# The even layer's q, k and convolution branch projected with the weight matrix as the stationary operand

## The chip, the cores and the metric

The kernel runs on one core of one Trainium2 chip. The metric is the time of one execution on the device in microseconds (us): the median of three runs of the kernel before is 798.65 us (798.03 to 799.74). A profiled execution gives a trace in which each engine's instructions stand with start and duration: PE (TensorE matmuls), PEld (TensorE loads of the stationary operand), DVE (VectorE), ACT (ScalarE), POOL (GpSimd) and SP (SyncE, which issues most of the transfers).

## The reference

Two layers act on 256 positions of width 2048. The even layer (the first) is the one that is changed:

```python
h = rms_norm(x, ev_norm_w[i])
proj = h @ w_in                              # 2048 -> 8192
q, k, v, g_ret, gate_b, gate_c, u, g_conv = jnp.split(proj, 8, axis=-1)   # 1024 columns each
q = rope(q.reshape(shp), pos)                # 4 heads of 256
k = rope(k.reshape(shp), pos)
o = retention_chunkwise(q, k, v.reshape(shp))
ret_out = rms_norm_nogain(o).reshape(b, s, RET_WIDTH) * jax.nn.silu(g_ret)
conv = lax.conv_general_dilated(gate_c * u, conv_w[:, None, :], ...)   # width 3, causal, per channel
conv_out = gate_b * conv * jax.nn.silu(g_conv)
return jnp.concatenate([ret_out, conv_out], axis=-1) @ w_out
```

The odd layer (RMS norm, a projection to 4608 columns, banded attention over 32 query heads with a gate, an output projection) is the same before and after.

## The kernel before

All inputs are float32. Every operand of a projection is split into two parts of the type float32r, a high one (a rounded copy) and a low one (what is left), and each product is made of three matmuls: high by high, high by low, low by high. The weights come from memory in pieces of 128 x 1024 float32 (two k-tiles of 512 columns). `Chunk.split` loads a piece (L164, issued by SP), makes the high part on ACT (L165, `wh`) and the low part on DVE (L166, `wl`). The activations, already split, lie in SBUF with features on the partitions: `a0h` and `a0l` are the normalised input of the even layer.

A `Chunk` is one block of 512 output columns: 16 k-tiles, two blocks of 128 positions, three products, so 96 matmuls (L143). In each, a 128 x 128 block of the activation is stationary and 512 columns of the weight piece move, so the result has positions on the partitions and 512 features beside them, in two PSUM tiles `ps..._0` and `ps..._1`, one for each block of positions. The even layer's input projection is 16 chunks, in the order of the table

```python
EVEN_ORDER = [4, 0, 2, 6, 5, 1, 3, 7, 10, 12, 14, 8, 11, 13, 15, 9]
```

where column block c belongs to kind c // 2 (0 q, 1 k, 2 v, 3 retention gate, 4 gate_b, 5 gate_c, 6 u, 7 g_conv) and half c % 2. After them come four chunks of the even output projection (`eo`), nine of the odd input projection (`okv`, `oq`, `og`) and four of the odd output projection (`oo`).

PE's instructions stand in the order in which the code makes them, except that a layer below may move one by a few rows. A chunk is fed piece by piece (`feed`), and after each piece one step of the queue `pending` is put in: work of the layer's other parts (rope, retention, convolution), written as generators. So short bursts of other PE work stand between the pieces of the projections.

`even_done` takes a finished chunk out of PSUM. Row scaling by `r0` (the RMS norm, one number for each position) is done there: ACT scales v and the gates on the way out (L383), DVE multiplies u by gate_c and gate_b by the gate (L387). For q and k, DVE makes the rope with tables that were multiplied by `r0` beforehand (L252), with positions on the partitions. But retention needs q and k with features on the partitions, and so does the convolution, which runs along positions. So `rope_turn` (L277) transposes each rope result on PE in four 128 x 128 pieces and ACT copies it to SBUF (L278), and `conv` transposes both of its inputs (`yt` L345, `bt` L362), which DVE then reads from PSUM. These transposes are matmuls with the identity (part of the table `cst`).

Of the kernel before, what the change touches and what calls it, by code (L numbers as in the profile page):

```python
# [8 lines left out]
F32 = mybir.dt.float32  # L9
F32R = mybir.dt.float32r  # L10
AF = mybir.ActivationFunctionType
ALU = mybir.AluOpType
# [3 lines left out]
P = 128  # L16
D = 2048
S = 256
T = S // P
KT = D // P  # L20
N = 512
PK = 2
NP = KT // PK
EPS = 1e-6
RH, RD = 4, 256
HD = 64
# [15 lines left out]
C_ROPE1 = C_LOWER + P  # L42
C_END = C_ROPE1 + T * 128
E_ROPE0 = 0
E_MASK = E_ROPE0 + T * 512
E_END = E_MASK + RH * 384

S_NW0 = 0
# [9 lines left out]
def hybrid_kernel(  # L58
# [13 lines left out]
    nc = tc.nc  # L72
# [4 lines left out]
    tw = ctx.enter_context(tc.tile_pool(name="tw", bufs=W2_BUFS))  # L77
    mm = ctx.enter_context(tc.tile_pool(name="mm", bufs=4, space=PSUM))
    tp = ctx.enter_context(tc.tile_pool(name="tp", bufs=2, space=PSUM))
    at = ctx.enter_context(tc.tile_pool(name="at", bufs=2, space=PSUM))  # L80

    cst = cp.tile([P, C_END], F32, tag="cst", name="cst")
# [43 lines left out]
    class Chunk:  # L126
# [30 lines left out]
        def split(self, pc, fine=False):  # L157
# [8 lines left out]
                nc.vector.tensor_tensor(out=wl[:, ws], in0=raw[:, ws], in1=f32(wh[:, ws]), op=ALU.subtract)  # L166
            return wh, wl

    def stage(chunks, done):

        q = 3 * NP // 4
        a, b = Chunk(*chunks[0]), Chunk(*chunks[1])
        a.feed(0, q)
        b.feed(0, q)
        drain()
        a.feed(q, NP)
        done(0, a.ps)
        b.feed(q, NP)
        done(1, b.ps)
        for n in range(2, len(chunks)):  # L180
            c = Chunk(*chunks[n])
            c.feed(0, NP)
            done(n, c.ps)
# [43 lines left out]

    with tc.tile_pool(name="e", bufs=1) as ep, tc.tile_pool(name="e2", bufs=2) as ep2:
        cst0 = ep.tile([P, E_END], F32, tag="cst0", name="cst0")
        rope0 = cst0[:, E_ROPE0 : E_ROPE0 + T * 512].rearrange("p (t a d) -> p t a d", t=T, a=2)  # L230
        r0 = cp.tile([P, T], F32, tag="r0", name="r0")
        ssx = cp.tile([P, T, 4], F32, tag="ssx", name="ssx")

# [12 lines left out]
            nc.vector.tensor_copy(r0, r)  # L246

        def load_tables():
            nc.sync.dma_start(out=cst0[:, :E_MASK], in_=const0[:, :E_MASK])
            for t in range(T):  # L250
                rt = cst0[:, E_ROPE0 + t * 512 : E_ROPE0 + (t + 1) * 512]
                nc.vector.tensor_scalar(out=rt, in0=rt, scalar1=r0[:, t : t + 1], scalar2=None, op0=ALU.mult)  # L252

        cact = Act("c0")

        def rope_pair(name, ps, dst):

            for t in range(T):
                v = ps[t].rearrange("p (h s d) -> p h s d", h=2, s=2)
                a = tw.tile([P, 2, 2, P], F32, tag="w2", name=f"ra{name}{t}")  # L260
                b = tw.tile([P, 2, 2, P], F32, tag="w2", name=f"rb{name}{t}")
                cs = rope0[:, t, 0].unsqueeze(1).broadcast_to([P, 2, 256])
                nc.vector.tensor_tensor(
                    out=a.rearrange("p h s d -> p h (s d)"),
                    in0=ps[t].rearrange("p (h d) -> p h d", h=2), in1=cs, op=ALU.mult,
                )
                for s in range(2):
                    sn = rope0[:, t, 1, s * P : (s + 1) * P].unsqueeze(1).broadcast_to([P, 2, P])
                    nc.vector.tensor_tensor(out=b[:, :, s, :], in0=v[:, :, 1 - s, :], in1=sn, op=ALU.mult)
                af = a.rearrange("p h s d -> p (h s d)")  # L270
                nc.vector.tensor_tensor(out=af, in0=af, in1=b.rearrange("p h s d -> p (h s d)"), op=ALU.add)
                pending.append(rope_turn(f"{name}{t}", af, dst[:, :, t * P : (t + 1) * P]))

        def rope_turn(name, a, dst):
            tr = tp.tile([P, 4, P], F32, tag="tp", name=f"rt{name}")
            for j in range(4):
                nc.tensor.transpose(tr[:, j, :], a[:, j * P : (j + 1) * P], ident)  # L277
            nc.scalar.activation(dst, tr, AF.Copy)  # L278
            yield

        def retention(i, qT, kT, v, sg):
            ch, cl = cact.new()
# [55 lines left out]
        def conv(i, y, bg):  # L338
            yield
            ch, cl = cact.new()  # L340
            for c in range(0, 4, 2):
                yt = tp.tile([P, 2, S], F32, tag="tp", name=f"yt{i}{c}")
                for j in range(2):
                    for t in range(T):
                        nc.tensor.transpose(  # L345
                            yt[:, j, t * P : (t + 1) * P], y[:, t, (c + j) * P : (c + j + 1) * P], ident
                        )
                a = tw.tile([P, 2, S], F32, tag="w2", name=f"ca{i}{c}")
                for j in range(2):
                    o = S_CONV + (4 * i + c + j) * 3  # L350
                    nc.vector.tensor_scalar(
                        out=a[:, j, :], in0=yt[:, j, :], scalar1=sml[:, o + 2 : o + 3], scalar2=None, op0=ALU.mult
                    )
                    for d in (1, 2):
                        nc.vector.scalar_tensor_tensor(
                            out=a[:, j, d:], in0=yt[:, j, : S - d], scalar=sml[:, o + 2 - d : o + 3 - d],
                            in1=a[:, j, d:], op0=ALU.mult, op1=ALU.add,
                        )
                bt = tp.tile([P, 2, S], F32, tag="tp", name=f"bt{i}{c}")
                for j in range(2):  # L360
                    for t in range(T):
                        nc.tensor.transpose(  # L362
                            bt[:, j, t * P : (t + 1) * P], bg[:, t, (c + j) * P : (c + j + 1) * P], ident
                        )
                nc.vector.tensor_tensor(out=a, in0=bt, in1=a, op=ALU.mult)
                ks = slice(c, c + 2)
                nc.scalar.activation(ch[:, ks, :], a, AF.Copy)
                nc.vector.tensor_tensor(out=cl[:, ks, :], in0=a, in1=f32(ch[:, ks, :]), op=ALU.subtract)
                yield
# [4 lines left out]
        def even_done(n, ps):  # L374
            kind, i = EVEN_ORDER[n] // 2, EVEN_ORDER[n] % 2
            if kind in (0, 1):
                dst = ep.tile([P, 4, S], F32, tag="qk"[kind], name=f"{'qk'[kind]}T{i}")
                rope_pair(f"{kind}{i}", ps, dst)
                keep[kind] = dst
            elif kind in (2, 3, 5, 7):  # L380
                dst = ep.tile([P, T, N], F32, tag={2: "v", 3: "g", 5: "v", 7: "g"}[kind], name=f"e{kind}{i}")
                for t in range(T):
                    nc.scalar.activation(  # L383
                        dst[:, t, :], ps[t], AF.Silu if kind in (3, 7) else AF.Copy, scale=r0[:, t : t + 1]
                    )
                keep[kind] = dst
                if kind == 3:  # L387
                    pending.append(retention(i, keep[0], keep[1], keep[2], keep[3]))
            else:
                dst = ep.tile([P, T, N], F32, tag="q" if kind == 6 else "k", name=f"e{kind}{i}")  # L390
                for t in range(T):
                    nc.vector.scalar_tensor_tensor(
                        out=dst[:, t, :], in0=ps[t], scalar=r0[:, t : t + 1],
                        in1=keep[5 if kind == 6 else 7][:, t, :], op0=ALU.mult, op1=ALU.mult,
                    )
                keep[kind] = dst
                if kind == 4:
                    pending.append(conv(i, keep[6], keep[4]))

        for n, c in enumerate(EVEN_ORDER):  # L400
            if n == 0:
                continue
            ch = Chunk(f"e{c}", w0, n, act0)
            if n == 1:
                ch.feed(0, 1)
                load_x(0)
                ch.feed(1, 3)
                load_x(1)
                ch.feed(3, 5)
                stats()  # L410
                even_done(0, ch0.ps)
                load_tables()
                ch.feed(5, 6)
                nc.sync.dma_start(out=cst, in_=const1)
                nc.vector.tensor_copy(identr, ident)
                ch.feed(6, NP)
                nc.sync.dma_start(out=cst0[:, E_MASK:], in_=const0[:, E_MASK:])
            else:
                ch.feed(0, NP)
            even_done(n, ch.ps)  # L420
# [401 lines left out]
def _constants():  # L822
# [3 lines left out]
    e, c = np.zeros((P, E_END), f), np.zeros((P, C_END), f)  # L826
    c[:, C_ID : C_ID + P] = np.eye(P, dtype=f)

    def rope(dst, o, d):
        inv = f(1.0) / (10000.0 ** (np.arange(0, d, 2) / d)).astype(f)  # L830
        a = (np.arange(S, dtype=f)[:, None] * inv[None, :]).astype(np.float64)
        cos, sin = np.cos(a).astype(f), np.sin(a).astype(f)
        full = np.concatenate([cos, cos, -sin, sin], 1)
        for t in range(T):
            dst[:, o + 2 * d * t : o + 2 * d * (t + 1)] = full[t * P : (t + 1) * P]

    rope(e, E_ROPE0, RD)
    rope(c, C_ROPE1, HD)
    j = np.arange(P)[:, None]
    i = np.arange(S)[None, :]  # L840
    for h in range(RH):
# [58 lines left out]
```

## Time and profile before

| | |
|---|---|
| median of three runs | 798.65 us |
| the profiled execution's own time | 798.12 us |
| its span, first to last instruction | 796.4 us |
| PE busy | 789.2 us, 99% of the span |
| weight loads (PEld) busy | 652.4 us, 82% |
| DVE busy | 500.0 us, 63% |
| ACT busy | 419.9 us, 53% |
| granted TensorE clock | full (1.0) throughout |

The page's busy time of PE counts an engine as busy while any matmul is in flight. Matmuls overlap: a 128 x 512 one lasts some 390 ns in the trace, while the next one starts some 227 ns after it. What a matmul costs is therefore the distance between starts, not the duration, and this is read from the timeline or from the chain of waits, where each piece is a run of instructions of one line with its length and count.

### The profile page before, as it was taken

To read this page: it belongs to the slowest core of one execution; us is meant where nothing else is said; L and a number is where in the kernel's file an instruction comes from. 1 tells how busy PE (TensorE), PEld (TensorE's weight loads), DVE (VectorE), ACT (ScalarE), POOL (GpSimd) and SP (SyncE) were. 2 spreads that over 40 slices of the span, in tenths; PEclk is the share of its full clock that TensorE was granted. 3 is DMA by queue.
4 is the path that set the end of the run, shared out by engine and by line. 5 is a ranking of instruction groups with operands and counts; after the bars stand their busy time and mean duration, and the time that the engine had idled before them with its cause. 6 is when DMAs were issued, how large, how long until landed. Compare 5 with 4: busy or idle time off the path is not lost.

```text
span 796.4 us, 10004 instructions
## 1 busy us (share of the span) xinstructions
PE 789.2 (99%) x3660; PEld 652.4 (82%) x3660; DVE 500.0 (63%) x742; ACT 419.9 (53%) x665; POOL 61.7 (8%) x61
## 2 busy tenths in 40 slices
PE   8999999999999999999999999999999999999998
PEld 5888888888888888888888888888888888888886
DVE  6676444664544475545857664877988877877651
ACT  6843444443444434343345444658758678686430
POOL 0000000000000000000000000330410501401000
PEclk9999999999999999999999999999999999999999
DMA  8966545555455555655555555463463464445750
GB/s 298 418 240 228 197 140 184 185 188 196 137 187 188 198 184 181 201 185 195 176 191 179 186 185 187 136 216 97 158 216 133 134 207 158 146 146 184 229 168 26
DMA packets 41088, 147.09 MB, mean 185 GB/s; under 512 B 4560, under 2 KB 4944, under 8 KB 40784
## 3 DMA queue, kind: packets, MB, share of 16 engines
q1 hardware_dynamic: 40752, 146.23, 54.3%
q8 instruction: 28, 0.46, 0.2%
q10 hardware_dynamic: 288, 0.24, 0.2%
q14 instruction: 20, 0.16, 0.1%
HBM read 144.36 MB, written 2.10 MB: 184 GB/s over the span
## 4 chain that ended last, share of the span: by engine, by line
PE 96%; POOL 1%; DVE 1%; DMA 1%; issue 0%; SPq 0%; ACT 0%; DVEq 0%; POOLq 0%
PE pse L143 44%; PE pseo L143 11%; PE psoo L143 11%; PE psoq L143 10%; PE psog L143 10%; PE psokv L143 3%; PE pt L675 1%; DMA we<-in_w 1%; PE ov L698 1%; PE ov L697 1%; POOL rq L225 1%; PE qt L598 1%; PE s L607 0%; PE s L610 0%; PE s L609 0%; PE gt L666 0%
## 5 line engine op out<-in xcount | busy, mean ns | idle before, releaser
L166 DVE TENSOR_TENSOR wle<-we,whe 128x1024 fp32r<-128x1024 f32 (+1 forms) x129 | 156.2, 1217 | 147.6 <-ACT whe L165 147.4
L165 ACT ACTIVATE whe<-we 128x1024 fp32r<-128x1024 f32 (+1 forms) x129 | 135.4, 1052 | 172.8 <-PE pse L143 160.5
L143 PE MATMUL pse<-whe,a0h 128*128 128x512 f32 x512 | 199.4, 394 | 1.4 <-ACT whe L165 1.4
L143 PE MATMUL pse<-whe,a0l 128*128 128x512 f32 x512 | 197.5, 390 | 0.0
L143 PE MATMUL pse<-wle,a0h 128*128 128x512 f32 x512 | 197.4, 389 | 0.0
L143 PEld LDWEIGHTS pse<-whe,a0h 128*128 128x128 f32 x512 | 95.8, 188 | 23.1 <-ACT whe L165 3.9
L143 PEld LDWEIGHTS pse<-whe,a0l 128*128 128x128 f32 x512 | 96.1, 188 | 20.5
L143 PEld LDWEIGHTS pse<-wle,a0h 128*128 128x128 f32 x512 | 96.2, 188 | 19.4
L165 ACT ACTIVATE wheo<-weo 128x1024 fp32r<-128x1024 f32 x32 | 33.9, 1061 | 48.3 <-PE pseo L143 32.7
L166 DVE TENSOR_TENSOR wleo<-weo,wheo 128x1024 fp32r<-128x1024 f32 x32 | 39.2, 1225 | 27.5 <-ACT wheo L165 27.5
L166 DVE TENSOR_TENSOR wloo<-woo,whoo 128x1024 fp32r<-128x1024 f32 x32 | 38.9, 1225 | 26.9 <-ACT whoo L165 26.7
L165 ACT ACTIVATE whoo<-woo 128x1024 fp32r<-128x1024 f32 x32 | 33.9, 1062 | 40.3 <-PE psoo L143 32.7
L165 ACT ACTIVATE whoq<-woq 128x1024 fp32r<-128x1024 f32 x32 | 34.0, 1063 | 36.3 <-PE psoq L143 14.0
L166 DVE TENSOR_TENSOR wloq<-woq,whoq 128x1024 fp32r<-128x1024 f32 x32 | 38.9, 1223 | 19.2 <-ACT whoq L165 18.7
L143 PE MATMUL psog<-whog,a1h 128*128 128x512 f32 x128 | 50.9, 398 | 0.0
L143 PE MATMUL psoq<-whoq,a1h 128*128 128x512 f32 x128 | 50.8, 397 | 0.0
L143 PE MATMUL pseo<-wheo,c0h 128*128 128x512 f32 x128 | 50.8, 397 | 0.0
L143 PE MATMUL psog<-wlog,a1h 128*128 128x512 f32 x128 | 50.0, 391 | 0.5 <-DVE wlog L166 0.5
L143 PE MATMUL psoo<-whoo,a2h 128*128 128x512 f32 x128 | 50.2, 392 | 0.0
L143 PE MATMUL psoq<-wloq,a1h 128*128 128x512 f32 x128 | 50.0, 391 | 0.0
L143 PE MATMUL psoo<-whoo,a2l 128*128 128x512 f32 x128 | 50.0, 390 | 0.0
L143 PE MATMUL psoq<-whoq,a1l 128*128 128x512 f32 x128 | 50.0, 390 | 0.0
(182 smaller groups left out, 1245.2 us busy)
## 6 DMA issues: line engine op xcount, KB each, us to landing
we<-in_w SPq DMA_DIRECT2D x127, 512.0 KB, 3.3
weo<-in_w SPq DMA_DIRECT2D x32, 512.0 KB, 3.3
woq<-in_w SPq DMA_DIRECT2D x32, 512.0 KB, 4.4
wog<-in_w SPq DMA_DIRECT2D x32, 512.0 KB, 3.4
woo<-in_w SPq DMA_DIRECT2D x32, 512.0 KB, 4.2
wokv<-in_w SPq DMA_DIRECT2D x8, 512.0 KB, 3.3
x<-in_xr SPq DMA_DIRECT2D x2, 1024.0 KB, 8.7
out_y<-y SPq DMA_DIRECT2D x7, 256.0 KB, 4.7
```

Source lines behind the costliest of these rows:

```text
L143: nc.tensor.matmul(self.ps[t], self.act(kt)[a][:, t * P : (t + 1) * P], w[:, k * N : (k + 1) * N], start=self.n[t] == 1, stop=self.n[t] == ...
L165: nc.scalar.activation(wh[:, ws], raw[:, ws], AF.Copy)
L166: nc.vector.tensor_tensor(out=wl[:, ws], in0=raw[:, ws], in1=f32(wh[:, ws]), op=ALU.subtract)
L225: nc.gpsimd.tensor_tensor(out=r, in0=v, in1=mhalf[:, :width], op=ALU.pow)
L598: nc.tensor.transpose(tr[:, h, :], qs[j][:, h].rearrange("p a d -> p (a d)"), identr)
L675: nc.tensor.transpose(tr[:, h, :], pr[j][:, h, t, :], ident)
L697: nc.tensor.matmul(of, v, ph, start=first, stop=False)
L698: nc.tensor.matmul(of, v, pl, start=False, stop=last)
```

## The change

Twelve of the sixteen chunks of the even input projection (all but kinds 2 and 3, v and the retention gate) become `Turned` chunks. In these a 128 x 128 block of the weights is stationary and all 256 positions of the activation move, so the result has features on the partitions: four blocks of 128 features with 256 positions each, two in each PSUM tile. A chunk is then 192 matmuls of 256 columns, not 96 of 512. The rope of q and k is done on DVE in this layout and written straight to `dst`. The convolution reads its inputs from SBUF, and its transposes are gone, as are `rope_turn` and its copy on ACT.

With features on the partitions, `r0` lies along the free axis. A new generator `rows` makes a tile `row` with `r0` in every partition (a diagonal matrix on DVE, one plain float32 matmul with a tile of ones, one copy on ACT), its square `row2`, and multiplies the rope tables by it. Those tables are 768 columns now (cosine, minus sine, sine over 256 positions), where they were 1024. The table `cst` (128 x 640, with the identity) is now loaded ahead of the sixth weight piece of the second chunk, directly before those rope tables; before, it came directly behind that piece.

The new chunk class:

```diff
+    class Turned(Chunk):
+        def __init__(self, name, w, c, act):
+            super().__init__(name, w, c, act)
+            self.ps = [p.rearrange("p (f q) -> p f q", f=2) for p in self.ps]
+
+        def products(self, pc, wh, wl, late=False):
+            for k in range(PK):
+                h, l = self.act(pc * PK + k)
+                for f in range(4):
+                    fs = slice(k * N + f * P, k * N + (f + 1) * P)
+                    for w, a in ((wh, h), (wh, l), (wl, h)):
+                        self.n[f // 2] += 1
+                        nc.tensor.matmul(
+                            self.ps[f // 2][:, f % 2], w[:, fs], a, start=self.n[f // 2] == 1,
+                            stop=pc == NP - 1 and k == PK - 1 and w is wl, skip_group_check=True,
+                        )
```

The tables and the row of `r0`:

```diff
         def load_tables():
+            nc.sync.dma_start(out=cst, in_=const1)
             nc.sync.dma_start(out=cst0[:, :E_MASK], in_=const0[:, :E_MASK])
+
+        def rows():
+            ones = tw.tile([P, P], F32, tag="w2", name="ones")
+            diag = tw.tile([P, S], F32, tag="w2", name="diag")
+            nc.vector.memset(ones, 1.0)
             for t in range(T):
-                rt = cst0[:, E_ROPE0 + t * 512 : E_ROPE0 + (t + 1) * 512]
-                nc.vector.tensor_scalar(out=rt, in0=rt, scalar1=r0[:, t : t + 1], scalar2=None, op0=ALU.mult)
+                nc.vector.tensor_scalar(
+                    out=diag[:, t * P : (t + 1) * P], in0=ident, scalar1=r0[:, t : t + 1], scalar2=None, op0=ALU.mult
+                )
+            yield
+            ps = tp.tile([P, S], F32, tag="tp", name="rowps")
+            nc.tensor.matmul(ps, ones, diag, start=True, stop=True)
+            nc.scalar.activation(row, ps, AF.Copy)
+            nc.vector.tensor_tensor(out=row2, in0=row, in1=row, op=ALU.mult)
+            nc.vector.tensor_tensor(
+                out=rope0, in0=rope0, in1=row.unsqueeze(1).broadcast_to([P, 3, S]), op=ALU.mult
+            )
+            yield
```

Rope, convolution, and the way out of PSUM:

```diff
         def rope_pair(name, ps, dst):
-            for t in range(T):
...
-                pending.append(rope_turn(f"{name}{t}", af, dst[:, :, t * P : (t + 1) * P]))
-
-        def rope_turn(name, a, dst):
-            tr = tp.tile([P, 4, P], F32, tag="tp", name=f"rt{name}")
-            for j in range(4):
-                nc.tensor.transpose(tr[:, j, :], a[:, j * P : (j + 1) * P], ident)
-            nc.scalar.activation(dst, tr, AF.Copy)
-            yield
+            for h in range(2):
+                x01 = ps[h]
+                b = tw.tile([P, 2, S], F32, tag="w2", name=f"rb{name}{h}")
+                out = dst[:, 2 * h : 2 * h + 2, :]
+                cs = rope0[:, 0].unsqueeze(1).broadcast_to([P, 2, S])
+                nc.vector.tensor_tensor(out=out, in0=x01, in1=cs, op=ALU.mult)
+                for i in range(2):
+                    nc.vector.tensor_tensor(out=b[:, i], in0=x01[:, 1 - i], in1=rope0[:, 1 + i], op=ALU.mult)
+                nc.vector.tensor_tensor(out=out, in0=out, in1=b, op=ALU.add)
...
             for c in range(0, 4, 2):
-                yt = tp.tile([P, 2, S], F32, tag="tp", name=f"yt{i}{c}")
-                for j in range(2):
-                    for t in range(T):
-                        nc.tensor.transpose(
-                            yt[:, j, t * P : (t + 1) * P], y[:, t, (c + j) * P : (c + j + 1) * P], ident
-                        )
...
-                bt = tp.tile([P, 2, S], F32, tag="tp", name=f"bt{i}{c}")
-                for j in range(2):
-                    for t in range(T):
-                        nc.tensor.transpose(
-                            bt[:, j, t * P : (t + 1) * P], bg[:, t, (c + j) * P : (c + j + 1) * P], ident
-                        )
-                nc.vector.tensor_tensor(out=a, in0=bt, in1=a, op=ALU.mult)
                 ks = slice(c, c + 2)
+                nc.vector.tensor_tensor(out=a, in0=bg[:, ks, :], in1=a, op=ALU.mult)
...
-            elif kind in (2, 3, 5, 7):
+            elif kind in (2, 3):
...
+                dst = ep.tile([P, 4, S], F32, tag={5: "v", 6: "q", 7: "g", 4: "k"}[kind], name=f"e{kind}{i}")
+                for b in range(2):
+                    d = dst[:, 2 * b : 2 * b + 2, :]
+                    if kind in (5, 7):
+                        by = (row2 if kind == 5 else row).unsqueeze(1).broadcast_to([P, 2, S])
+                    else:
+                        by = keep[5 if kind == 6 else 7][:, 2 * b : 2 * b + 2, :]
+                    nc.vector.tensor_tensor(out=d, in0=ps[b], in1=by, op=ALU.mult)
+                    if kind == 7:
+                        nc.scalar.activation(d, d, AF.Silu)
+                        nc.vector.tensor_tensor(out=d, in0=d, in1=by, op=ALU.mult)
...
-            ch = Chunk(f"e{c}", w0, n, act0)
+            ch = (Chunk if c // 2 in (2, 3) else Turned)(f"e{c}", w0, n, act0)
```

On PE, the start of the second chunk (q) is this before, one k-tile of 512 columns: `whe`, `wle` are the high and low weights, `a0h`, `a0l` those of the activation, `pse` the result, and the size is that of the moving operand's result.

```order
L143 MATMUL pse_0_298<-whe_0_301,a0h_93 128x512
L143 MATMUL pse_0_298<-wle_0_302,a0h_93 128x512
L143 MATMUL pse_0_298<-whe_0_301,a0l_94 128x512
L143 MATMUL pse_1_299<-whe_0_301,a0h_93 128x512
L143 MATMUL pse_1_299<-wle_0_302,a0h_93 128x512
L143 MATMUL pse_1_299<-whe_0_301,a0l_94 128x512
```

After, the same place on PE, and the same k-tile:

```order
L184 MATMUL pse_0_300<-a0h_93,whe_0_303 128x256
L184 MATMUL pse_0_300<-a0l_94,whe_0_303 128x256
L184 MATMUL pse_0_300<-a0h_93,wle_0_304 128x256
L184 MATMUL pse_0_300<-a0h_93,whe_0_303 128x256
L184 MATMUL pse_0_300<-a0l_94,whe_0_303 128x256
L184 MATMUL pse_0_300<-a0h_93,wle_0_304 128x256
L184 MATMUL pse_1_301<-a0h_93,whe_0_303 128x256
L184 MATMUL pse_1_301<-a0l_94,whe_0_303 128x256
L184 MATMUL pse_1_301<-a0h_93,wle_0_304 128x256
L184 MATMUL pse_1_301<-a0h_93,whe_0_303 128x256
L184 MATMUL pse_1_301<-a0l_94,whe_0_303 128x256
L184 MATMUL pse_1_301<-a0h_93,wle_0_304 128x256
```

Six matmuls of 512 columns became twelve of 256, each with a weight load of its own.

On PE in the third chunk (k), before: a rope transpose of q between two pieces' matmuls (`rt` the transposed tile, `ra` the rope result).

```order
L143 MATMUL pse_0_491<-whe_1_518,a0h_93 128x512
L143 MATMUL pse_0_491<-wle_1_519,a0h_93 128x512
L143 MATMUL pse_0_491<-whe_1_518,a0l_94 128x512
L277 MATMUL rt_511<-cst,ra_479 128x128 x4
L143 MATMUL pse_1_492<-whe_1_518,a0h_93 128x512
L143 MATMUL pse_1_492<-wle_1_519,a0h_93 128x512
```

After, between the second and the third chunk stands the one new matmul that makes `row`, and no transpose follows in the third:

```order
L184 MATMUL pse_1_301<-a0h_241,whe_7_549 128x256
L184 MATMUL pse_1_301<-a0l_242,whe_7_549 128x256
L184 MATMUL pse_1_301<-a0h_241,wle_7_550 128x256
L285 MATMUL rowps<-diag,ones 128x256
L184 MATMUL pse_0_595<-a0h_93,whe_0_598 128x256
L184 MATMUL pse_0_595<-a0l_94,whe_0_598 128x256
```

The bursts of four transposes left PE's stream; the matmul of `rows` entered it once.

On DVE, the way out of PSUM of the first g_conv chunk (kind 7) in the kernel after, between the low parts of the next chunk's pieces:

```order
L166 TENSOR_TENSOR wle_3_2750<-we_3_2748,whe_3_2749 128x1024
L412 TENSOR_TENSOR e_2649<-pse_0_2407,row_296 128x512
L412 TENSOR_TENSOR e_2649<-pse_1_2408,row_296 128x512
L166 TENSOR_TENSOR wle_4_2780<-we_4_2778,whe_4_2779 128x1024
L415 TENSOR_TENSOR e_2649<-e_2649,row_296 128x512 x2
L166 TENSOR_TENSOR wle_5_2810<-we_5_2808,whe_5_2809 128x1024
```

Before, DVE had no part in it; ACT took that chunk out in two instructions, between the high parts:

```order
L165 ACTIVATE whe_2_2065<-we_2_2064 128x1024
L165 ACTIVATE whe_3_2083<-we_3_2082 128x1024
L383 ACTIVATE e_2023<-pse_0_1877,r_296 128x512
L383 ACTIVATE e_2023<-pse_1_1878,r_296 128x512
L165 ACTIVATE whe_4_2101<-we_4_2100 128x1024
```

The scaling of gate_c and g_conv moved from ACT to DVE, and g_conv takes two more multiplications there.

More of the change, by code (lines that the diff above doesn't have):

```diff
@@ L44 @@
 E_ROPE0 = 0
-E_MASK = E_ROPE0 + T * 512
+E_MASK = E_ROPE0 + 3 * S
 E_END = E_MASK + RH * 384
@@ L229, in hybrid_kernel @@
         cst0 = ep.tile([P, E_END], F32, tag="cst0", name="cst0")
-        rope0 = cst0[:, E_ROPE0 : E_ROPE0 + T * 512].rearrange("p (t a d) -> p t a d", t=T, a=2)
+        rope0 = cst0[:, E_ROPE0:E_MASK].rearrange("p (a q) -> p a q", a=3)
+        row, row2 = (ep.tile([P, S], F32, tag=f"row{i}", name=f"row{i}") for i in range(2))
         r0 = cp.tile([P, T], F32, tag="r0", name="r0")
@@ L254, in hybrid_kernel @@
         cact = Act("c0")
         def rope_pair(name, ps, dst):
-            for t in range(T):
[L259 to L265, printed above, removed]
-                )
[L267 to L271, printed above, removed]
-                pending.append(rope_turn(f"{name}{t}", af, dst[:, :, t * P : (t + 1) * P]))
@@ L351, in conv @@
                     nc.vector.tensor_scalar(
-                        out=a[:, j, :], in0=yt[:, j, :], scalar1=sml[:, o + 2 : o + 3], scalar2=None, op0=ALU.mult
+                        out=a[:, j, :], in0=y[:, c + j, :], scalar1=sml[:, o + 2 : o + 3], scalar2=None, op0=ALU.mult
                     )
@@ L355, in conv @@
                         nc.vector.scalar_tensor_tensor(
-                            out=a[:, j, d:], in0=yt[:, j, : S - d], scalar=sml[:, o + 2 - d : o + 3 - d],
+                            out=a[:, j, d:], in0=y[:, c + j, : S - d], scalar=sml[:, o + 2 - d : o + 3 - d],
                             in1=a[:, j, d:], op0=ALU.mult, op1=ALU.add,
                         )
-                bt = tp.tile([P, 2, S], F32, tag="tp", name=f"bt{i}{c}")
-                for j in range(2):
-                    for t in range(T):
-                        nc.tensor.transpose(
-                            bt[:, j, t * P : (t + 1) * P], bg[:, t, (c + j) * P : (c + j + 1) * P], ident
-                        )
-                nc.vector.tensor_tensor(out=a, in0=bt, in1=a, op=ALU.mult)
                 ks = slice(c, c + 2)
+                nc.vector.tensor_tensor(out=a, in0=bg[:, ks, :], in1=a, op=ALU.mult)
                 nc.scalar.activation(ch[:, ks, :], a, AF.Copy)
@@ L379, in even_done @@
                 keep[kind] = dst
-            elif kind in (2, 3, 5, 7):
-                dst = ep.tile([P, T, N], F32, tag={2: "v", 3: "g", 5: "v", 7: "g"}[kind], name=f"e{kind}{i}")
+            elif kind in (2, 3):
+                dst = ep.tile([P, T, N], F32, tag="vg"[kind - 2], name=f"e{kind}{i}")
                 for t in range(T):
                     nc.scalar.activation(
-                        dst[:, t, :], ps[t], AF.Silu if kind in (3, 7) else AF.Copy, scale=r0[:, t : t + 1]
+                        dst[:, t, :], ps[t], AF.Silu if kind == 3 else AF.Copy, scale=r0[:, t : t + 1]
                     )
@@ L389, in even_done @@
             else:
[L390 to L395, printed above, removed]
+                dst = ep.tile([P, 4, S], F32, tag={5: "v", 6: "q", 7: "g", 4: "k"}[kind], name=f"e{kind}{i}")
[9 more added lines that the diff above has]
+                        nc.vector.tensor_tensor(out=d, in0=d, in1=by, op=ALU.mult)
                 keep[kind] = dst
@@ L412, in hybrid_kernel @@
                 load_tables()
-                ch.feed(5, 6)
-                nc.sync.dma_start(out=cst, in_=const1)
+                pending.append(rows())
+                ch.feed(5, 6, steps=0)
                 nc.vector.tensor_copy(identr, ident)
@@ L827, in _constants, with angles @@
     c[:, C_ID : C_ID + P] = np.eye(P, dtype=f)
-    def rope(dst, o, d):
+    def angles(d):
         inv = f(1.0) / (10000.0 ** (np.arange(0, d, 2) / d)).astype(f)
         a = (np.arange(S, dtype=f)[:, None] * inv[None, :]).astype(np.float64)
[L832 to L838, printed above, removed]
+        return np.cos(a).astype(f), np.sin(a).astype(f)
+    cos, sin = angles(RD)
+    e[:, E_ROPE0:E_MASK] = np.concatenate([cos.T, -sin.T, sin.T], 1)
+    cos, sin = angles(HD)
+    full = np.concatenate([cos, cos, -sin, sin], 1)
+    for t in range(T):
+        c[:, C_ROPE1 + 2 * HD * t : C_ROPE1 + 2 * HD * (t + 1)] = full[t * P : (t + 1) * P]
     j = np.arange(P)[:, None]
```

## The prediction

> **What bounds the kernel now.** I read the page's busy times first, then the waits of PE, then the chain of work that ended last.
>
> ```profile
> span 796.4 us, 10004 instructions
> PE 789.2 (99%) x3660; PEld 652.4 (82%) x3660; DVE 500.0 (63%) x742; ACT 419.9 (53%) x665; POOL 61.7 (8%) x61
> PEclk9999999999999999999999999999999999999999
> PE 96%; POOL 1%; DVE 1%; DMA 1%; issue 0%; SPq 0%; ACT 0%; DVEq 0%; POOLq 0%
> PE warm L195 <- DVE zero L192: 1.5, 1, 1.5
> PE pse L143 <- ACT whe L165: 1.4, 2, 0.9
> PE psog L143 <- DVE wlog L166: 0.5, 1, 0.5
> ```
>
> PE is the bound: it is busy for 99% of the span at the full clock, the chain lies on it for 96%, and in all it waited 3.4 us for others (the last three rows), none of it in the chunks that change. So the time moves with what PE's stream costs. That is not the sum of durations, which overlap, but the distance from one start to the next, and two rows give it for the matmul that the change replaces. From the chain of work, start, length and what:
>
> ```profile
> 214.38 76.21 PE pse L143 x336
> 297.93 76.20 PE pse L143 x336
> ```
>
> 336 matmuls of 512 columns in 76.2 us are 226.8 ns each, twice to the digit, with the whole of loading, splitting and emptying of chunks beside them. This is the price of one old matmul.
>
> **The matmuls that are replaced.** Twelve chunks of 96 are 1152 matmuls of 512 columns; after, they are 2304 of 256. The columns that stream are the same, so the question is what a matmul costs besides its columns. The kernel has the new form already, in the odd layer's scores: float32r, a 128 x 128 stationary block, 256 columns, two products in a row into the same result. The timeline of PE there, and of the weight loads beside it:
>
> ```profile
> 535.97 0.40 PE L607 MATMUL s<-kT,q1T 128*128 128x256 f32 x2
> 536.20 0.28 PE L609 MATMUL s<-kT,q1T 128*128 128x256 f32 x1
> 536.32 0.28 PE L610 MATMUL s<-kT,q1T 128*128 128x256 f32 x1
> 536.44 0.28 PE L609 MATMUL s<-kT,q1T 128*128 128x256 f32 x1
> 536.56 0.28 PE L610 MATMUL s<-kT,q1T 128*128 128x256 f32 x1
> 536.68 0.40 PE L143 MATMUL psoq<-whoq,a1h 128*128 128x512 f32 x1
> ...
> 536.20 0.19 PEld L610 LDWEIGHTS s<-kT,q1T 128*128 128x128 f32 x1
> 536.32 0.19 PEld L609 LDWEIGHTS s<-kT,q1T 128*128 128x128 f32 x1
> ```
>
> The last four of the six start 0.12 us apart, and the first two take 0.23 together (535.97 to 536.20). I take 120 ns, since a long stream looks like the end of this burst and not like its start. A second reason: 226.8 less 120 is 106.8 ns for 256 columns, so 512 columns are 213.6 and 13 ns are left over for each matmul, and 256 columns with the same 13 are again 120. So 2304 x 0.120 = 276.5 us against 1152 x 0.2268 = 261.3: **+15.2 us**. The ends for the range are 113.4 ns (half of 226.8, near the 115 of the first two), which makes this term 0, and 125 ns (one step of 5 above the 120, for a stream far longer than six), which makes it +26.7.
>
> **The Trainium skill at this place.** The page "TensorE: Matmul & The Clock Gate", section "Back-to-back issue gap", gives a warm matmul N/2.4 + 2.5 ns. By it 512 columns would be 215.8 ns and 256 would be 109.2, and this term would be 1152 x 2.5 = +2.9 us. The trace disagrees at 512 columns, with 226.8 ns.
>
> **The transposes that go.** The rope's are eight bursts of four on PE (L277), the convolution's four groups each of `yt` (L345) and `bt` (L362):
>
> ```profile
> L277 PE MATMUL rt<-cst,ra 128*128 128x128 f32 x32 | 4.8, 271 | 0.0
> L345 PE MATMUL yt<-cst,e 128*128 128x128 f32 x16 | 2.4, 272 | 0.0
> L362 PE MATMUL bt<-cst,e 128*128 128x128 f32 x16 | 2.5, 276 | 0.0
> ...
> 149.07 0.44 PE rt L277 x4
> 149.50 2.79 PE pse L143 x12
> 152.29 0.44 PE rt L277 x4
> 152.72 19.10 PE pse L143 x84
> 171.82 0.44 PE rt L277 x4
> ...
> 290.59 0.44 PE yt L345 x4
> 291.47 4.10 PE pse L143 x18
> 295.57 0.44 PE yt L345 x4
> 296.00 1.40 PE pse L143 x6
> 297.40 0.53 PE bt L362 x4
> ```
>
> From 149.07 to 171.82 are 22.75 us with 96 matmuls of 512 columns (21.77 us at 226.8 ns), so two rope bursts cost 0.98 us, or 0.49 each with what they leave behind; eight cost 3.9. The convolution's from 290.59 to 297.93 (where the run of 336 above begins) are 7.34 us with 24 such matmuls (5.44), so 1.90, and twice that is 3.8. All of it lies on PE's chain: **-7.7 us**.
>
> **The new matmul of `rows`.** One plain float32 matmul of 128 x 256. The retention has such, and each shows as two records:
>
> ```profile
> 201.22 0.43 PE ro L306 x2
> 202.51 8.21 PE pse L143 x36
> ```
>
> 0.43 us, and 36 matmuls behind such a group take 8.21 where 8.16 are due: **+0.5 us**. Its bounds are 0.4 and 0.6.
>
> **What lies beside PE, costed at nothing.** DVE and ACT in the stretch of plain chunks, and the second chunk's weights (ACT's timeline), with the matmul that uses the first of them:
>
> ```profile
> 214.40:290.00 75.60, 75.60 (x335) 62.55 (x335) 37.35 (x33) 32.28 (x33) 0.00 (x0) 1.00 0.59 194
> ...
> L263 DVE TENSOR_TENSOR ra<-pse,cst 128x512 f32<-128x512 f32 x8 | 5.5, 684 | 3.9 <-PE pse L143 3.9
> L383 ACT ACTIVATE e<-pse,r 128x512 f32<-128x512 f32 x16 | 10.8, 687 | 6.8 <-PE pse L143 6.8
> ...
> 38.69 1.06 ACT L165 ACTIVATE whe<-we 128x1024 fp32r<-128x1024 f32 x1 [0.45 <-DMA we<-in_w]
> 45.46 0.39 PE L143 MATMUL pse<-whe,a0h 128*128 128x512 f32 x1
> ```
>
> In the window's row the columns after the window are its length, then the busy us of PE, PEld, DVE, ACT and POOL: DVE is busy 37 of 76 us, ACT 32. Eight of the sixteen L383 leave ACT (four SiLU come back there, on SBUF), and DVE gets eight for gate_c and g_conv, and four more multiplications of g_conv: 12 x 0.68 = 8.2 us over some 180 us of the branch. The rope keeps its four DVE operations of the same sizes for each half. The eight copies behind the rope's transposes leave ACT. The two scalings of the rope table become one, with two small operations for the diagonal, one for `row2` and a copy on ACT. A chunk takes some 22 us and its two PSUM tiles aren't needed again before the next but one begins, so an emptying that is late by a microsecond holds nothing. Were that cover gone, the price would be the 0.68 us of one such DVE operation before a chunk; twelve times that is 8 us.
>
> On SP's queue, the load of `cst` moves ahead of the sixth weight piece of the second chunk (it stood behind it) and the rope table gets smaller. The seventh piece is the one that is waited for there: ACT takes it at 38.69 after a wait of 0.45 us, done at 39.75, and PE uses it at 45.46. Those 5.7 us hide the move. The matmul of `rows` waits for the diagonal on DVE, behind `r0`; queued behind it on PE is the whole third chunk. But it stands behind all of the second chunk's matmuls, and DVE makes `diag` ahead of the low parts of that chunk's last three pieces, which PE has by then used. No new wait.
>
> **The sum.** 15.2 - 7.7 + 0.5 = +8.0 us. The profiled execution took 798.12 us (span 796.4 and 1.7 around it), so 806.1; the median of the three runs is 0.5 higher, so **806.6 us**, 1.0% slower.
>
> **Rivals.**
>
> *Faster: the 256-column matmul costs half the 512-column one.* If the first two of each burst show the true rate (115 ns and down to 113.4) and the 120 belongs to something that passes, as after a wait, then the first term is 0 and the sum is -7.2: 791.5 us. For it: the pair's 0.23 us. Against: four starts 0.12 apart at the end of the burst, and the line through 512 and 256 columns above. The sign turns where the first term eats the 7.2 us up, at 113.4 + 7200 / 2304 = 116.5 ns. 12%. The formula of the Trainium skill quoted above leans to this side too, with 798.65 + 2.9 - 7.2 = 794.4 us; of the 12%, 3 are for that.
>
> *Slower by more: weight loads become the bound.* After the change there is a load for every 256 columns. A load lasts 188 ns (the 0.19 of the rows above). If loads could not overlap at all, 2304 x 0.188 = 433 us would replace 261.3, and the time would be near 963 us. Against: in the burst the loads start 0.12 apart, each 0.19 long, so they overlap. But six in a row are all that the trace has; a stream of 192 could run dry of what was prepared ahead, at 123 to 130 ns: 2304 x 0.003 = 7 to 23 us on top, 814 to 830 us. 12%.
>
> The Trainium skill speaks against the change here: "Trainium Kernel Development and Optimization", "Performance Expectations", takes the busy share of the weight loads as a good metric for the distance from the limit, where that of matmuls is a bad one. By it 652.4 us, plus 1152 loads of 0.188 less 64 of 0.14, would be 860 us and more than the span. The trace disagrees, in the loads that overlap from 536.20 on.
>
> *A new wait takes more than the transposes gave:* say the row of `r0` comes late and PE stands at the matmul that makes it. With the 5.7 us of slack above I give this 2%; it would add its lateness, some 2 to 6 us, to 806.6.
>
> **How the numbers follow.** The main case (118.5 to 121.5 ns, 803 to 810 us) gets 70%, the faster rival 12%, the one with more cost 12%, the wait 2%, and 4% lie between main case and faster rival (797 to 803). A measurement of this kernel tells a change from none at about 0.2%, 1.6 us. So faster 0.13, same 0.03, slower 0.84. The range from 800 to 816 leaves out the faster rival and the upper part of the costlier one, some 20%. The main case alone has 803 to 810.
>
> **What would show it.** After, L184 has 2304 matmuls and starts 0.120 us apart in the timeline; a chunk of 192 takes 23.0 us where one of 96 took 21.8. No L277, L345 or L362. PE waits for no more than now. If starts in the middle of a chunk stand 0.113 apart, the faster rival is right, and the kernel with it; if they stand 0.125 or more apart, the weight loads are. If PE's waits grew instead, the costing beside PE is wrong.

## The result, and the profile after

The changed kernel takes 806.76 us (median of four runs, 805.83 to 807.62); the kernel before, run beside it, 799.19. The ratio is 1.0098, with a 95% interval from 1.0085 to 1.0111: slower by 7.6 us. Forecast were 806.6 us and 1.0%.

The page of the changed kernel, with PE's waits and, of the chain of work, the pieces that answer to those shown of before (start, length, what):

```profile
span 804.7 us, 12183 instructions
PE 797.1 (99%) x4750; PEld 706.9 (88%) x4750; DVE 506.8 (63%) x757; ACT 413.5 (51%) x654; POOL 61.7 (8%) x61
PE 96%; POOL 1%; DVE 1%; DMA 1%; issue 0%; ACT 0%; SPq 0%; DVEq 0%; POOLq 0%
L184 PE MATMUL pse<-a0h,whe 128*128 128x256 f32 x768 | 217.8, 284 | 0.0
PE pse L143 <- ACT whe L165: 1.8, 2, 1.4
PE warm L215 <- DVE zero L212: 1.5, 1, 1.5
PE psog L143 <- DVE wlog L166: 0.5, 1, 0.5
...
29.78 23.04 PE pse L184 x192
52.82 0.43 PE rowps L285 x2
53.26 23.02 PE pse L184 x192
217.30 167.04 PE pse L184 x1392
```

PE is still busy for 99% and the chain still lies on it for 96%. The last row shows the main term: 1392 matmuls of 256 columns in 167.04 us, which is 120.0 ns each, over seven chunks and a quarter with no other work between them. A chunk takes 23.04 us, and the matmul that makes `row` 0.43. PE waits 3.8 us where it waited 3.4, all of it where it waited before, at the start and in the odd layer. In the timeline of PE the starts in the middle of a chunk stand as evenly as a row can print:

```profile
130.01 0.28 PE L184 MATMUL pse<-a0l,whe 128*128 128x256 f32 x1
130.13 0.28 PE L184 MATMUL pse<-a0h,wle 128*128 128x256 f32 x1
130.25 0.28 PE L184 MATMUL pse<-a0h,whe 128*128 128x256 f32 x1
130.37 0.28 PE L184 MATMUL pse<-a0l,whe 128*128 128x256 f32 x1
```

### The profile page after: what moved, and what is told of

It is laid out like the page before. It is cut to its first block, busy times and chain, and to the rows that moved or that the text cites. A ratio compares the mean times of both kernels' runs of the same rounds, so it can differ in the third digit from the quotient of the medians.

```text
span 804.7 us, 12183 instructions
## 1 busy us (share of the span) xinstructions
PE 797.1 (99%) x4750; PEld 706.9 (88%) x4750; DVE 506.8 (63%) x757; ACT 413.5 (51%) x654; POOL 61.7 (8%) x61
## 4 chain that ended last, share of the span: by engine, by line
PE 96%; POOL 1%; DVE 1%; DMA 1%; issue 0%; ACT 0%; SPq 0%; DVEq 0%; POOLq 0%
PE pse L184 34%; PE psoo L143 11%; PE pseo L143 11%; PE pse L143 11%; PE psoq L143 10%; PE psog L143 10%; PE psokv L143 3%; PE pt L695 1%; PE ov L718 1%; PE ov L717 1%; DMA we<-in_w 1%; POOL rq L245 1%; PE qt L618 1%; PE s L627 0%; PE s L630 0%; PE s L629 0%
## 5 line engine op out<-in xcount | busy, mean ns | idle before, releaser
L184 PE MATMUL pse<-a0h,whe 128*128 128x256 f32 x768 | 217.8, 284 | 0.0
L184 PE MATMUL pse<-a0l,whe 128*128 128x256 f32 x768 | 217.2, 283 | 0.0
L184 PE MATMUL pse<-a0h,wle 128*128 128x256 f32 x768 | 217.2, 283 | 0.0
L184 PEld LDWEIGHTS pse<-a0h,whe 128*128 128x128 f32 x768 | 147.4, 192 | 0.2
L184 PEld LDWEIGHTS pse<-a0l,whe 128*128 128x128 f32 x768 | 147.4, 192 | 0.2
L184 PEld LDWEIGHTS pse<-a0h,wle 128*128 128x128 f32 x768 | 147.3, 192 | 0.0
L143 PE MATMUL pse<-whe,a0h 128*128 128x512 f32 x128 | 48.9, 397 | 1.8 <-ACT whe L165 1.8
```

The costliest lines, as they stand in the source:

```text
L143: nc.tensor.matmul(self.ps[t], self.act(kt)[a][:, t * P : (t + 1) * P], w[:, k * N : (k + 1) * N], start=self.n[t] == 1, stop=self.n[t] == ...
L184: nc.tensor.matmul(self.ps[f // 2][:, f % 2], w[:, fs], a, start=self.n[f // 2] == 1, stop=pc == NP - 1 and k == PK - 1 and w is wl, skip_ ...
```

## The experiments

The theory (A) is that a float32r matmul costs its columns at 2.4 per ns (256 columns in 226.8 - 120.0 = 106.8 ns, as the prediction has it) and 13.3 ns besides, whichever operand is stationary, so that more and narrower matmuls are the whole loss and the transposes the whole gain. The rivals put the loss on the turned roles (weights as the stationary operand), on the weight loads, or on an issue rate.

### Narrow matmuls without the turn

In the kernel before, each matmul of thirteen chunks is cut in two: of the twelve that the change turns and of the even layer's first chunk as well. That one holds columns of v, but it is named `e0`, and the test goes by the name:

```diff
+            self.halves = name[0] == "e" and name[1] != "o" and int(name[1:]) // 2 not in (2, 3)
...
-                nc.tensor.matmul(
-                    self.ps[t], self.act(kt)[a][:, t * P : (t + 1) * P], w[:, k * N : (k + 1) * N],
+                wd = N // 2 if self.halves else N
+                for lo in range(0, N, wd):
+                    nc.tensor.matmul(
+                        self.ps[t][:, lo : lo + wd], self.act(kt)[a][:, t * P : (t + 1) * P],
+                        w[:, k * N + lo : k * N + lo + wd],
```

> The kernel before, with activations stationary as they were and all transposes kept, but in the twelve chunks that the change turns each matmul of 512 columns is made as two of 256 with the same stationary block. Theory A (a matmul of float32r costs its columns and some 13 ns besides, whichever operand is stationary): 2304 x 120 ns for 1152 x 226.8 ns, +15.2 us, about 814 us; starts 0.120 apart in L143 of those chunks. Rival B (the extra cost of the change belongs to the weights as stationary operand, which ACT and DVE have just written): no more than before, 799 us.

It took 814.38 us, ratio 1.0196 (1.0182 to 1.0210), so +15.5 us on its own kernel before (798.84). The 15.2 of A are for twelve chunks; for thirteen, 1248 x 13.2 ns, they are 16.5 (the spans of the two profiled executions, 812.9 and 796.4 us, differ by 16.5). From its groups of instructions (the other two products have 832 as well: 3 x 832 are 13 x 192) and from its chain of work:

```profile
L146 PE MATMUL pse<-whe,a0h 128*128 128x256 f32 x832 | 167.6, 286 | 0.6 <-ACT whe L169 0.6
...
221.67 67.92 PE pse L146 x566
```

566 in 67.92 us are 120.0 ns again, with the activation stationary and the weights moving. The first chunk is told apart from the twelve by the timeline of PE: the start of the second chunk and that of the even output projection, in the kernel before, in this one and in the changed one (x2 in a row merges two matmuls).

```profile
29.14 0.39 PE L143 MATMUL pse<-whe,a0h 128*128 128x512 f32 x1
373.97 0.39 PE L143 MATMUL pseo<-wheo,c0h 128*128 128x512 f32 x1
...
30.70 0.40 PE L146 MATMUL pse<-whe,a0h 128*128 128x256 f32 x2
390.28 0.40 PE L146 MATMUL pseo<-wheo,c0h 128*128 128x512 f32 x1
...
29.62 0.28 PE L184 MATMUL pse<-a0h,whe 128*128 128x256 f32 x1
384.17 0.40 PE L143 MATMUL pseo<-wheo,c0h 128*128 128x512 f32 x1
```

Between these two starts lie the other three chunks of v and the gate and all of the twelve: 344.83 us before, 359.58 here, so the twelve alone cost 14.8 where A gave 15.2. So the loss is the width, not the turn, and rival B falls. The changed kernel takes 354.55 there, 5.0 less than this one, and 420.5 us from the second start to the end of the span where this one takes 422.6, 2.1 less (the transposes of the convolution's second half stand there). Together 7.1 us: that is what the transposes, less the matmul of `rows`, are worth (forecast 7.7 - 0.5 = 7.2). The 7.6 us between the medians of the two kernels hold the first chunk as well.

The extra matmuls bring extra loads: this kernel has 4908 of each, the changed one 4750 of each. So the 13.3 ns are the price of a matmul with its load, and no run tells the two apart.

### Half as wide again

```diff
-                        nc.tensor.matmul(
-                            self.ps[f // 2][:, f % 2], w[:, fs], a, start=self.n[f // 2] == 1,
+                        for t in range(T):
+                            ts = slice(t * P, (t + 1) * P)
+                            nc.tensor.matmul(
+                                self.ps[f // 2][:, f % 2, ts], w[:, fs], a[:, ts],
```

> The changed kernel with each of its 2304 matmuls of 256 columns made as two of 128 with the same stationary block. Theory A (13 ns for each matmul beside its columns): 128 columns are 53.4 + 13.3 = 66.7 ns, 4608 of them 307 us, +31 on the changed kernel, about 838 us. Theory C (the 120 ns are the time of one weight load, which bounds every matmul of 256 columns or fewer): 4608 x 120 = 553 us, +276, about 1083 us. Theory D (an issue rate bounds short matmuls, as the eight 128-column transposes of L598 that take 0.63 us, 79 ns each, or 86 in the steady part): 4608 x 79 to 86 ns, +88 to +120, about 895 to 927 us.

It took 1043.94 us in a single run, some 237 us more than the changed kernel. None of the three theories had the number. From the chain of work, and the weight loads in the timeline:

```profile
214.42 36.18 PE pse L186 x324
...
220.00 0.30 PEld L186 LDWEIGHTS pse<-a0h,wle 128*128 128x128 f32 x2
220.22 0.30 PEld L186 LDWEIGHTS pse<-a0h,whe 128*128 128x128 f32 x2
220.44 0.30 PEld L186 LDWEIGHTS pse<-a0l,whe 128*128 128x128 f32 x2
```

324 in 36.18 us are 111.7 ns, for half the columns of the 120 ns matmul. Two loads come every 0.22 us, 0.11 apart, each lasting 0.19. So there is a floor of some 112 ns, and the 256-column matmul stands just above it. A's sum of columns and 13.3 ns holds only over that floor (it gives 66.7 here). C came nearest (+276 for +237) and was still wrong: if the floor were 120, this stream would take 120 as well. A general issue rate is not the floor, since the float32r transposes in the kernel before, as many instructions each, go faster. From its timeline and its groups of instructions:

```profile
526.36 0.80 PE L598 MATMUL qt<-identr,qs 128*128 128x128 f32 x8
526.99 0.47 PE L143 MATMUL psog<-whog,a1h 128*128 128x512 f32 x1
...
L598 PEld LDWEIGHTS qt<-identr,qs 128*128 128x128 f32 x64 | 6.3, 140 | 1.0
L277 PEld LDWEIGHTS rt<-cst,ra 128*128 128x128 f32 x32 | 4.0, 140 | 1.0
```

The eight go at 79 ns on the mean and at 85 to 89 once the burst runs, with loads that last 140 ns and not 190. That would fit a floor set by the loads. But the rope's float32 transposes (L277) have loads of the same 140 ns and take 0.44 us for four, 0.11 each, so the length of a load does not set the distance by itself. What makes the floor of 112 ns stays open.

### One part of the change at a time

Two kernels that differ from the changed one in which chunks are turned, with the code of the kernel before for the others:

```diff
-            ch = (Chunk if c // 2 in (2, 3) else Turned)(f"e{c}", w0, n, act0)
+            ch = (Turned if c // 2 in (0, 1) else Chunk)(f"e{c}", w0, n, act0)
```

> Only q and k turned (four chunks); the convolution branch with its transposes as before. If the terms add up: 384 pairs x 13.2 ns = +5.1, eight rope bursts -3.9, the matmul of rows +0.5, so +1.7 us on the kernel before. If the turned chunks cost something that the sum doesn't hold (or give something), it differs from that by more than 0.8 us.

```diff
-            ch = (Chunk if c // 2 in (2, 3) else Turned)(f"e{c}", w0, n, act0)
+            ch = (Turned if c // 2 >= 4 else Chunk)(f"e{c}", w0, n, act0)
```

> Only the convolution branch turned (eight chunks); rope with its transposes as before. If the terms add up: 768 pairs x 13.2 ns = +10.1, the convolution's transposes -3.8, the matmul of rows +0.5, so +6.8 us on the kernel before; with the kernel that turns only q and k, less the 0.5 that both pay, this is the +8.0 of the whole change.

Against 798.84 us of the kernel before, q and k alone took 800.41 (ratio 1.0020, 1.0011 to 1.0029), +1.6 where 1.7 were due; the convolution branch alone 805.27 (1.0081, 1.0067 to 1.0095), +6.4 where 6.8 were due. Together, less the 0.5 that both pay, 7.5, and the whole change measured 7.6. The terms add up to within the 1 us or so that these intervals leave, and no larger stall hides between them.

### Wide matmuls in the turned layout

If width is the loss, the features can lie on the partitions without it: high and low activation side by side make 512 columns for the high weights.

```diff
+                    nc.tensor.matmul(
+                        self.bank[f], wh[:, fs], self.act.pair(kt), start=kt == 0, stop=False, skip_group_check=True
+                    )
+                    nc.tensor.matmul(
+                        self.bank[f][:, :S], wl[:, fs], h, start=False, stop=kt == KT - 1, skip_group_check=True
+                    )
...
+                        nc.scalar.activation(x01[:, f], self.bank[f][:, S:], AF.Copy)
+                        nc.vector.tensor_tensor(out=x01[:, f], in0=self.bank[f][:, :S], in1=x01[:, f], op=ALU.add)
```

> The same twelve chunks with features on the partitions and no transposes, but the high and the low activation lie side by side, so that one matmul of 512 columns makes high weights by both (in two halves of a PSUM bank that ACT and DVE add on the way out) and one of 256 columns makes low weights by high. Weights come in the order of 256-column halves of a chunk. Theory A (13 ns for each matmul beside its columns): 768 x (226.8 + 120) = 266.3 us for 261.3 before, +5.0, transposes -7.7, rows +0.5: -2.2 us on the kernel before, about 797 us. Rival (weights as stationary operand cost something beside the number of matmuls, or the sums on the way out make PE wait): at the kernel before or above it.

> The joined form for q and k only, the convolution branch as before. Theory A: 256 x 346.8 ns = 88.8 us for 87.1, +1.7, rope's transposes -3.9, rows +0.5: -1.7 us on the kernel before, so the convolution branch is worth 0.5 us more or less. Rival as for the joined form of all twelve chunks: no gain.

All twelve chunks took 800.74 us against 798.89 (ratio 1.0023, 1.0014 to 1.0032), +1.9 where -2.2 were due: a miss of 4 us. Q and k alone took 798.29 (0.9989, 0.9980 to 0.9998), -0.6 where -1.7 were due. In the form of all twelve PE waited no longer (3.2 us in all), so it is the stream. The timeline of PE in the form of all twelve (L196 is the wide one, L199 the narrow):

```profile
231.30 0.40 PE L196 MATMUL pse<-a,whe 128*128 128x512 f32 x1
231.54 0.28 PE L199 MATMUL pse<-a,wle 128*128 128x256 f32 x1
231.66 0.40 PE L196 MATMUL pse<-a,whe 128*128 128x512 f32 x1
231.89 0.28 PE L199 MATMUL pse<-a,wle 128*128 128x256 f32 x1
232.01 0.40 PE L196 MATMUL pse<-a,whe 128*128 128x512 f32 x1
232.24 0.28 PE L199 MATMUL pse<-a,wle 128*128 128x256 f32 x1
232.36 0.40 PE L196 MATMUL pse<-a,whe 128*128 128x512 f32 x1
```

Three pairs take 1.06 us (231.30 to 232.36), 353 ns a pair and not 346.8, and 406 pairs in a row give the same; the wide ones take 0.23 to 0.24. Over 768 pairs that is 5.0 us. Where does it come from, the order or the joined operand? The same kernel with the order changed, and two streams that leave products out:

```diff
+            for low in range(2):
+                for k in range(4):
...
+                        if low == 0:
...
+                        else:
```

> As the joined form of all twelve chunks, whose trace shows 353 ns for a pair of 512 and 256 columns where 346.8 were due; here each piece's eight matmuls of 512 columns come first and then its eight of 256. Theory E (a wide matmul pays some 6.7 ns more where a narrow one stands before it): eight such places in a piece become one, with a tail of about 30 ns as behind the score bursts: 24 to 47 ns less a piece, 96 pieces, 2.3 to 4.5 us below the joined form's 800.7, so 796.2 to 798.4 us. Theory F (the 512 columns of the joined operand cost 233 ns by themselves): no change, 800.7 us.

> The joined form of all twelve chunks without the products of the low weights (those 768 matmuls are left out, so the output lacks them): a stream of 512 columns alone, with the weights stationary. Theory E: starts 0.2268 apart, 768 of them 174.2 us, 97.2 us below the joined form. Theory F: 0.233 apart, 179 us.

> The same stream with 384 columns moving (high part and half of the low part; the rest and the low weights' products are left out). Theory A (columns at 2.4 per ns and 13.3 ns besides): 173.3 ns. A cost in proportion to the columns (226.8 x 384 / 512): 170.1 ns, as it would also be 113.4 at 256, where 120 were measured.

> The same grouping for q and k only, 32 pieces. Theory E: 0.8 to 1.5 us below the joined form of q and k (0.6 below the kernel before), so 1.4 to 2.1 us below the kernel before. Theory F: 0.6 below it, as ungrouped.

From the chains of work, the first two rows of the grouped form (L197 wide, L202 narrow), the third of the stream of 512 columns alone; last, from the timeline of PE, the stream of 384:

```profile
230.51 1.84 PE pse L197 x8
233.31 1.84 PE pse L197 x8
...
214.39 70.72 PE pse L195 x312
...
129.68 3.28 PE L195 MATMUL pse<-a,whe 128*128 128x384 f32 x18
```

Grouped, a piece of eight and eight takes 2.80 us (230.51 to 233.31), where 2.77 were due and 2.83 came when they alternated. The time fell to 797.87 us against 798.98, ratio 0.9992 (0.9983 to 1.0001), 2.9 us below the alternating form, in the 2.3 to 4.5 of theory E. The stream of 512 columns alone goes at 70.72 / 312 = 226.7 ns with the joined operand and weights stationary, so F falls: it is the mixing of widths that costs.

The cost is not in the first wide matmul behind a narrow one alone. Over 85 grouped pieces in the trace the wide ones start 233, 236, 228, 232 and 231 ns apart before they settle at 227, and the first narrow one behind them takes 113, 7 less than the rest. The kernel before shows the same where other products and other result tiles follow each other: behind the score burst that the prediction shows, the matmuls of 512 columns start 233, 236 and 229 ns apart (from 536.68 us).

The kernel with the stream of 512 columns takes 707.40 us in a single run, 93.3 less than the alternating form where 97.2 were due; its PE waits for high parts in the first turned chunks, which the faster stream uses up too early:

```profile
PE pse L195 <- ACT whe L167: 3.2, 2, 1.7
```

Those 3.2 us are most of the difference. The stream of 384 has its last end 3.28 us after its first start; less one duration of 0.334 that is 17 distances of 173.3 ns, which is A's number to the digit and not the 170.1 of proportion. (That kernel, 688.64 us in a single run, waits for its weights in places, 12.3 us for the high parts; these 18 stand between waits.)

Grouped for q and k alone, the time is 797.60 us, ratio 0.9985 (0.9976 to 0.9994): the lowest of the kernels that make all products, 1.4 us below the kernel before, where E gave 1.4 to 2.1. Its edge on the alternating form of q and k, 0.7 us, is too small for these intervals to tell from none.

## Why the prediction was right

*The replaced matmuls* (+15.2): the 120 ns that were read off the last four of six score matmuls held over 2304, and the cut of the old kernel gives +14.8 by itself over the same twelve chunks. Here the choice was between 113.4 and 125, and the reason that decided it was the end of the burst and the line through two widths. A third width, 384 columns, now lies on that line: 512, 384 and 256 columns at 226.7, 173.3 and 120.0 ns, 53.3 apart for each 128.

*The transposes* (-7.7) and *the matmul of `rows`* (+0.5): together 7.2, measured 7.1 between two kernels of equal matmul widths in the twelve chunks. The matmul itself shows 0.43 us.

*The sum* (+8.0): from the start of the second chunk to the end of the span the two traces differ by 9.7 - 1.9 = +7.8 us, and the medians by 7.6. That the time itself came within 0.2 us of the forecast is in part luck: the kernel before ran 0.5 us higher beside the changed one than on its own, and the change was 0.4 smaller than forecast.

*Costed at nothing*: PE's waits rose by 0.4 us, at the start, where the first weights land and nothing was changed; the same wait is anything from 0.5 to 1.8 us in the kernels above. DVE rose by 6.8 us to 506.8, and PE waited for it no more than before. No wait of PE appeared behind the move on SP's queue.

*The faster rival* is out: the first two of each burst at 115 ns were the passing part. The changed kernel's first turned chunk begins in the same way, behind matmuls of 512 columns: its first two starts are 113 and 119 ns from the next, and the rest 120. The formula of the Trainium skill's page "TensorE: Matmul & The Clock Gate", "Back-to-back issue gap", cited for it, which that section gives for an isolated matmul, misses at all three widths of these streams: by it they would be 215.8, 162.5 and 109.2 ns.

*The rival of the weight loads* was wrong for this change, but only just: there is a floor at 112 ns, 8 under the 120, though no run shows that the loads make it. By the Trainium skill's rule cited for it, the busy share of the loads ("Trainium Kernel Development and Optimization", "Performance Expectations"), the loads came to 860 us. The trace disagrees: overlapping loads count once, and the share is 706.9 us or 88%.

The step that would have failed is one that the prediction didn't need: that 512 and 256 columns may be added up in any order. The joined form showed 6.5 ns a pair more when they alternate.

## What to carry to other kernels

Before turning a matmul's roles for a better layout, count the matmuls and not the columns: where PE is the bound, a change of layout pays the fixed cost of every extra matmul and its load, here 13.3 ns together, and 1152 of them outweighed 64 transposes in bursts of four at about 0.49 us. Look in the trace for a run of the new form, however short, and read distances between starts from its end: here the first two were 113 and 119 ns, and all behind them 120. And if the layout is wanted, win the width back first: for q and k, wide matmuls in the turned layout, grouped by width, made the same idea a small gain.

## What the runs showed of the hardware

Starts of float32r matmuls with a 128 x 128 stationary block of their own, in even streams: 226.7 ns at 512 columns, 173.3 at 384, 120.0 at 256, and 111.7 at 128, which lies on a floor and not on the line of the other three; what makes the floor stays open. Streams of mixed widths cost more than the sum: 353 ns for an alternating pair of 512 and 256, 2.80 us for eight and eight in a row, for sums of 346.8 ns and 2.77 us. The extra is spread over the first five wide matmuls behind the narrow ones; why they pay stays open.
